# A hybrid encoder block on one core: keys taken in pairs, the second pass held back, expert rows spaced anew

## The chip, the core and the metric

The kernel runs on one core of a Trainium2 chip. The metric is the device time of one execution in microseconds (us). The engines are named as the profile names them: TensorE is PE (its weight loads PEld), VectorE is DVE, ScalarE is ACT, GpSimd is POOL, and SyncE (SP) issues most transfers.

## What is computed

The reference, cut to its frame (one layer, 1024 tokens of 1024 columns, 256 memory tokens, all float32):

```python
x = x + hybrid_mixer(rmsnorm(x))               # gated delta rule, 4 heads | RG-LRU, 512 channels
x = x + memory_cross_attention(rmsnorm(x), rmsnorm(mem))
x = x + peer_ffn(rmsnorm(x))                   # below
out = rmsnorm(x)

q = (t @ wq).reshape(ntok, 8, 2, 128)          # peer_ffn: 8 heads, two half queries
sc = einsum('thpd,hpkd->thpk', q, subkeys)     # 128 sub-keys per half
s1, i1 = top_k(sc[:, :, 0], 16); s2, i2 = top_k(sc[:, :, 1], 16)
best, pos = top_k(all sums of s1 and s2, 16)   # 16 experts per head, 128 per token
idx = e1 * 128 + e2; gate = softmax(best)
out = sum over the 128 experts of gate * gelu(u_tab[idx] . t) * v_tab[idx]
```

The expert tables `u` and `v` have 16384 rows of 4 KB each.

## The kernel before

**Two ways to the experts.** For 512 of the tokens (256 to 767) the kernel goes through all experts densely: a gate matrix G (token x expert, mostly zero) is built, then for each of 128 keys j (128 experts each) the `hidden(j)` step multiplies the tokens with `u`, applies gelu and the gates, and the `out(j)` step multiplies the result with `v` into PSUM. float32 products are made as three products of a high and a low part (`split`, `mm3`): ACT casts the high part (`uh`, `vh`, `dah`), DVE subtracts it (`ul`, `vl`, `dal`). The other 512 tokens, in four blocks of 128, fetch their experts: `fetch()` issues an indirect transfer on POOL that brings one expert row of 4 KB to each of 128 tokens (tile `rb`, 6 places), and `step()` lets DVE work on it (one pass over 128x1024: a dot product for `u`, a scaled sum for `v`). There are 4 blocks x 128 experts x 2 tables = 1024 such steps, called expert rows here.

**Stages.** The mixers run in four passes of 256 tokens (`heads`: projections, convolutions, the RG-LRU; `delta`: the chunked delta rule, a chain of small products). The units of `attend` (0, 128, 256, 512, 768) follow as their tokens are done: cross attention, the expert query, scores (16 rounds of `top16`), then `choose`/`select`, which gives the expert numbers `idx`. When the mixers are over, `gates` builds G for the dense tokens: per four tokens DVE writes two one-hot tiles (`oh1`, `oh2`), ACT scales one by the gates (`ohg`), PE multiplies them (`gd`), ACT copies to `stage`, and each 16 tokens a transfer of 1 MB writes `stage` to memory. The rest of `attend` runs beside it. Then the dense stage runs alone with the expert rows that are left.

**What sets the order.** `together` interleaves these streams by ranks and by a planner's clock while the program is written; each engine then runs its instructions in that order. PE's hook `tick` calls `step()` once per `pe.pace` nanoseconds of planned PE time, but not while DVE is planned more than `SLACK` behind or the oldest row has not landed: `PACES` are the spacings in the four passes, `PACE_G` that of the gates stage, and in the dense stage the rows that are left are spread evenly (`DENSE / rows left`). In `heads` a pass starts its projections when the pass before has finished its RG-LRU:

```python
while prev and "y" not in prev.ready:
    yield None
```

**The dense stage.** PSUM has one bank for `dh` (the hidden product), six for the outputs of three token blocks, and one (`po3`) for the fourth block, which is used for two keys and half the columns at a time (`last(0)`, `last(1)` in `out` of an odd key) and each time added to `acc` by DVE before PE may write the bank again. G lies as [128 experts, 512 tokens, 8 keys], so the gates of one key are read with a stride of 8 floats.

Of the kernel before, what the change touches and what calls it, by code (L numbers as in the profile page):

```python
# [8 lines left out]
F = mybir.dt.float32  # L9
BF = mybir.dt.bfloat16  # L10
FR = mybir.dt.float32r
I32 = mybir.dt.int32
U32 = mybir.dt.uint32
AF = mybir.ActivationFunctionType
# [9 lines left out]
TD = 2 * T  # L24
EC = 8
# [11 lines left out]
HOP, SLACK, WAIT = 100.0, 8000.0, 1000.0  # L37
SHARE = (6.0, 1.0, 6.0, 1.0)
L_NORM, L_STEP, L_CONV, L_SOFT, L_GATE = 14000.0, 2500.0, 4000.0, 6000.0, 1500.0
PACES = (2800.0, 2800.0, 2800.0, 3500.0)  # L40
PACE_G, DENSE = 3500.0, 1316000.0
FIRST = 0
EARLY = T
UNITS = ((0, 1), (128, 1), (256, 2), (512, 2), (768, 2))
# [5 lines left out]
def block_kernel(ctx: ExitStack, tc: tile.TileContext, a):  # L50
# [76 lines left out]
    act, dve = Engine(nc.scalar, 200.0, 0.72), Engine(nc.vector, 68.0, 1.04)  # L127
# [296 lines left out]
    def heads(fp, P, prev, qkv):  # L424

        t0, ready = P.t0, P.ready
# [11 lines left out]
        def tmp():  # L438
            return fp.tile([128, T], F, name="cy", bufs=CB)

        while prev and "y" not in prev.ready:
            yield None
        pe.pace = PACES[t0 // T]
        hT = fp.tile([128, 8, T], F, name="hT", bufs=1)
# [330 lines left out]

    done = {}
    read, chosen = set(), set()


    def attend(fp, t0, nb, KT, VM):  # L780
# [72 lines left out]
        for r in range(16):  # L853
            qT = ahead
            if r < 15:
                ahead = yield from query(r + 1)
            yield [qT]
            sk = fp.tile([128, 128], F, name="subk", bufs=2)
            sp.dma_start(sk, a["subk"][r])
            sc = bank("sc", 2)  # L860
            for b in range(nb):
                pe.matmul(sc[:, b * 128:(b + 1) * 128], qT[:, b * 128:(b + 1) * 128], sk,
                          start=True, stop=True)
            sc = sc.rearrange("p (b k) -> p b k", b=4)
            for b in range(nb):
                top16(fp, s12[b][:, r, :], i12[b][:, r, :], sc[:, b, :], 128)
            yield 0

        def choose():
            if not t0:  # L870
# [162 lines left out]
    def u_raw(p, j):  # L1033
        raw = p.tile([128, D], F, name="ur", bufs=2)
        sp.dma_start(raw, a["ut"][j])
        return raw

    def v_raw(p, j):
        raw = p.tile([128, D], F, name="vr", bufs=2)
        sp.dma_start(raw, a["v"][j * 128:(j + 1) * 128, :])  # L1040
        return raw

    def dense(p1, p, ps, hT, raws):
        hhi, hlo = hT
        NT = TD // 128
        res = [[ps.tile([128, 512], F, name=f"po{t}{d}") for d in range(2)] for t in range(NT - 1)]
        acc = p.tile([128, D], F, name="acc", bufs=1)
        row3 = D0 + TD - 128
        sp.dma_start(acc, x2d[row3:row3 + 128, :])

        def split(raw, name, bufs):
            hi = p1.tile([128, D], FR, name=name + "h", bufs=bufs)
            lo = p1.tile([128, D], FR, name=name + "l", bufs=bufs)
            act.copy(hi, raw)
            dve.tensor_sub(lo, raw, hi.bitcast(F))
            return hi, lo

        G = [None]
        A, V = {}, {}

        def hidden(j):
            if j % EC == 0:
                G[0] = p.tile([128, TD, EC], F, name="G", bufs=2)
                sp.dma_start(G[0], gd[j // EC])
            u, v = raws.pop(0) if raws else (u_raw(p1, j), v_raw(p1, j))
            uh, ul = [c8(t) for t in split(u, "u", 2)]
            V[j] = split(v, "v", 3)
            h = ps.tile([128, TD], F, name="dh")
            for c in range(8):
                mm3(h, (uh[:, c, :], ul[:, c, :]), (hhi[:, c, :], hlo[:, c, :]), c == 0, c == 7)  # L1070
            g = p.tile([128, TD], F, name="dg", bufs=2)
            act.activation(g, h, AF.Gelu_apprx_tanh)
            dve.tensor_mul(g, g, G[0][:, :, j % EC])
            ah = p.tile([128, TD], FR, name="dah", bufs=3)
            al = p.tile([128, TD], FR, name="dal", bufs=3)
            act.copy(ah, g)
            dve.tensor_sub(al, g, ah.bitcast(F))
            A[j] = (ah, al)

        xs = []  # L1080

        def add_res(t):
            x = xs[0][:, t, :]
            for d in range(2):
                ds = slice(d * 512, (d + 1) * 512)
                dve.tensor_add(x[:, ds], x[:, ds], res[t][d])
            finish(x, D0 + t * 128, xs[0][:, NT - 1, :])

        def out(j):
            def part(o, i, t, d, start, stop):  # L1090
                ts, ds = slice(t * 128, (t + 1) * 128), slice(d * 512, (d + 1) * 512)
                mm3(o, [x[:, ts] for x in A[i]], [x[:, ds] for x in V[i]], start, stop)

            def last(d):
                o = ps.tile([128, 512], F, name="po3")
                for i in (j - 1, j):
                    part(o, i, NT - 1, d, i < j, i == j)
                ds = slice(d * 512, (d + 1) * 512)
                dve.tensor_add(acc[:, ds], acc[:, ds], o)

            if j == 124:
                xs.append(p.tile([128, TD, EC], F, name="G", bufs=2).rearrange("p (t d) k -> p t (d k)", t=4))
                sp.dma_start(xs[0][:, 0:NT - 1, :],
                             x2d[D0:row3, :].rearrange("(t p) m -> p t m", p=128))
            if j % 2:
                last(0)
            for t in range(NT - 1):
                for d in range(2):
                    part(res[t][d], j, t, d, j == 0, j == 127)
                if j == 127:  # L1110
                    add_res(t)
            if j % 2:
                last(1)
                for i in (j - 1, j):
                    A.pop(i), V.pop(i)

        hidden(0)
        for j in range(128):
            if j + 1 < 128:
                hidden(j + 1)  # L1120
            for _ in range(LATE):
                next(late[0], None)
            out(j)
        finish(acc, row3, xs[0][:, NT - 1, :])
# [161 lines left out]
    def attended():  # L1286
        yield from memory(att, KT, VM)
        first.rank = FIRST
        for t0, nb in UNITS:
            while t0 not in done:  # L1290
                yield None
            yield from attend(att, t0, nb, KT, VM)
        while D0 + TD - T not in begun:
            yield None
        front.close()
        d1 = ctx.enter_context(tc.tile_pool(name="duv", bufs=1))
        dn.append(d1)
        raws.extend((u_raw(d1, j), v_raw(d1, j)) for j in range(2))

    dn, hT, raws, begun = [], [], [], set()  # L1300
    wp = front.enter_context(tc.tile_pool(name="wp", bufs=1))
    att = front.enter_context(tc.tile_pool(name="att", bufs=1))
    KT = att.tile([128, 8, MEM], F, name="KT")
# [4 lines left out]
    with tc.tile_pool(name="dn", bufs=1, side="right") as d2, \  # L1308
            tc.tile_pool(name="dps", bufs=1, space=bass.MemoryType.PSUM) as dps:
        pe.pace, pe.real = DENSE / (2.0 * (S - TD) - stepped[0]), False  # L1310
        dense(dn[0], d2, dps, hT, raws)
    while step():
        pass

# [63 lines left out]
```

## Time and profile before

| | us |
|---|---|
| median of 3 runs | 3226.76 (3224.28 to 3238.54) |
| the profiled execution, its own time | 3238.51 |
| its span, first to last instruction | 3236.7 |
| span up to the first expert row, about | 430 |
| mixers with expert rows, up to the gates stage | 430 to 1305 |
| gates stage | 1305 to 1743 |
| dense stage, first to last product | 1743 to 3223 |

A window of the profile gives, for each engine, its busy time and in brackets the number of its instructions that began there; PEclk is the granted TensorE clock as a share of full speed. "A <- B" in a list of waits means that A stood idle until B was done.

### The profile page before, as it was taken

What the parts mean: (1) busy time and instruction counts of PE and PEld (TensorE: products, weight loads), DVE (VectorE), ACT (ScalarE), POOL (GpSimd) and SP (SyncE); (2) the same over time, 40 slices, a digit from 0 to 9 for tenths busy, and PEclk for the clock granted to TensorE, in tenths of its full rate; (3) what the DMA queues carried; (4) which work ended last, traced back from release to release, by engine and by line L of the source; (5) the groups of instructions that cost most, each with busy time, mean ns of one, the idle gap of its engine ahead of it and who ended that gap; (6) DMA issues with size and microseconds to landing.
All of it is one profiled execution on the core that took longest, in us unless ns stands there. A gap on an engine that the chain in (4) does not pass through costs nothing.

```text
span 3236.7 us, 46492 instructions
## 1 busy us (share of the span) xinstructions
PE 2982.7 (92%) x16212; PEld 2554.5 (79%) x16212; DVE 2723.6 (84%) x5999; ACT 1281.2 (40%) x2694; POOL 1454.7 (45%) x1046
## 2 busy tenths in 40 slices
PE   7899899899999889888667999999999999999998
PEld 6889888888898788777566778778877778788786
DVE  7652578888786987999997999888999999899999
ACT  6844264255315531656575322222222232222222
POOL 0000023245232443343423776666666666666673
PEclk9999999999999999998778999999999999999999
DMA  5244769888787778889978899999999989999996
GB/s 172 92 150 144 228 235 323 307 303 307 274 293 252 249 284 303 295 302 302 308 249 289 303 354 326 339 325 342 355 350 339 344 313 360 325 343 353 345 347 211
DMA packets 321547, 941.66 MB, mean 291 GB/s; under 512 B 28912, under 2 KB 108832, under 8 KB 319264
## 3 DMA queue, kind: packets, MB, share of 16 engines
q0 software_dynamic: 148048, 538.04, 46.8%
q1 hardware_dynamic: 107216, 367.08, 31.5%
q10 hardware_dynamic: 66048, 33.56, 3.7%
q8 instruction: 128, 2.10, 0.3%
q14 instruction: 107, 0.88, 0.1%
HBM read 894.53 MB, written 44.04 MB: 290 GB/s over the span
## 4 chain that ended last, share of the span: by engine, by line
PE 49%; DVE 25%; DMA 12%; issue 7%; ACT 5%; POOL 2%; SPq 0%; another core or an unknown queue 0%; DVEq 0%; POOLq 0%; ACTq 0%
PE dh L108 15%; PE po L108 14%; PE pj L108 14%; DVE rb L83 8%; PE gd L108 4%; DMA rb<-in_v,idx 4%; DVE oh L83 3%; DMA gd<-stage 2%; POOL rb L1157 2%; DMA rb<-in_u,idx 2%; PE tp L113 1%; DVE i L83 1%; DMA w<-in_pwq 1%; PE sc L108 1%; DVE dg L83 1%
## 5 line engine op out<-in xcount | busy, mean ns | idle before, releaser
L1157 POOL DMA_INDIRECT rb<-in_u,idx x512 | 701.2, 1369 | 1104.2 <-DVE lxf L83 419.7
L1157 POOL DMA_INDIRECT rb<-in_v,idx x512 | 744.5, 1454 | 638.8 <-DVE rb L83 429.7
L83 DVE SCALAR_TENSOR_TENSOR rb<-rb,ga 128x1024 f32<-128x1024 f32 x512 | 655.8, 1281 | 29.5 <-DMA rb<-in_v,idx 23.9
L83 DVE SCALAR_TENSOR_TENSOR rb<-rb 128x1024 f32<-128x1024 f32 x512 | 611.2, 1218 | 31.4 <-DMA rb<-in_u,idx 31.3
L108 PE MATMUL pj<-hT,w 128*128 128x256 f32 (+1 forms) x2880 | 591.4, 357 | 16.0 <-DMA w<-in_pwq 14.4
L108 PEld LDWEIGHTS pj<-hT,w 128*128 128x128 f32 x2880 | 491.0, 195 | 70.8 <-DMA w<-in_pwq 14.5
L108 PE MATMUL po<-vh,dah 128*128 128x512 f32 x1024 | 408.5, 399 | 27.7 <-DVE acc L83 27.7
L108 PE MATMUL dh<-hT_h,uh 128*128 128x512 f32 x1024 | 409.9, 400 | 7.6 <-ACT dg L83 6.9
L108 PE MATMUL dh<-hT_h,ul 128*128 128x512 f32 x1024 | 408.3, 399 | 2.1 <-DVE ul L83 2.1
L108 PE MATMUL dh<-hT_l,uh 128*128 128x512 f32 x1024 | 408.5, 399 | 0.0
L108 PE MATMUL po<-vl,dah 128*128 128x512 f32 x1024 | 408.1, 399 | 0.0
L108 PE MATMUL po<-vh,dal 128*128 128x512 f32 x1024 | 406.8, 398 | 0.0
L83 ACT CAST uh<-ur 128x1024 fp32r<-128x1024 f32 x128 | 134.7, 1053 | 602.2 <-PE dh L108 399.8
L108 PE MATMUL gd<-ohg,oh 128*128 128x128 f32 x1024 | 182.7, 335 | 83.3 <-ACT ohg L83 66.1
L108 PEld LDWEIGHTS po<-vh,dah 128*128 128x128 f32 x1024 | 193.4, 189 | 80.4 <-DVE acc L83 33.4
L108 PEld LDWEIGHTS gd<-ohg,oh 128*128 128x128 f32 x1024 | 165.9, 234 | 99.7 <-ACT ohg L83 91.8
L108 PEld LDWEIGHTS dh<-hT_h,uh 128*128 128x128 f32 x1024 | 195.2, 191 | 56.2 <-ACT dg L83 7.8
L108 PEld LDWEIGHTS dh<-hT_h,ul 128*128 128x128 f32 x1024 | 194.4, 190 | 50.6 <-DVE ul L83 2.9
L108 PEld LDWEIGHTS dh<-hT_l,uh 128*128 128x128 f32 x1024 | 195.0, 190 | 47.4
L108 PEld LDWEIGHTS po<-vl,dah 128*128 128x128 f32 x1024 | 193.8, 189 | 47.1
L108 PEld LDWEIGHTS po<-vh,dal 128*128 128x128 f32 x1024 | 193.7, 189 | 46.8
L83 ACT CAST dah<-dg 128x512 fp32r<-128x512 f32 x128 | 79.6, 622 | 305.1 <-DVE dg L83 302.4
(341 smaller groups left out, 4806.0 us busy)
## 6 DMA issues: line engine op xcount, KB each, us to landing
ur<-in_ut SPq DMA_DIRECT2D x128, 512.0 KB
vr<-in_v SPq DMA_DIRECT2D x128, 512.0 KB
w<-in_wA SPq DMA_DIRECT2D x80, 512.0 KB
w<-in_pwq SPq DMA_DIRECT2D x80, 512.0 KB
gd<-stage ACTq DMA_DIRECT2D x32, 1024.0 KB
G<-gd SPq DMA_DIRECT2D x16, 2048.0 KB
w<-in_wout SPq DMA_DIRECT2D x40, 512.0 KB
w<-in_wq SPq DMA_DIRECT2D x40, 512.0 KB
```

The costliest lines, as they stand in the source:

```text
L83: r = call(*args, **kw)
L108: self.engine.matmul(out, l, r, **kw)
L113: self.engine.transpose(out, i, ident)
L1157: pool.indirect_dma_start(out=t, out_offset=None, in_=a[ph], in_offset=bass.IndirectOffsetOnAxis(ap=B["idx"][:, k:k + 1], axis=0))
```

## The change

Three edits:

1. Keys in pairs: the gelu of two neighbouring keys is written side by side (`dg` is [512 tokens, 2]), and the product with G, the cast `dah` and the difference `dal` are made once per pair. `hidden` now runs two keys ahead of `out`, and the split of `v` is a step of its own (`values`), one key ahead.
2. The expert rows' spacing: 2800, 2800, 2800, 3500 ns become 2500, 2500, 2500, 3000 in the passes, and 3500 becomes 5000 in the gates stage.
3. The projections of the second pass wait until some unit has had its 16 rounds of scores (`asked`), which is the first unit (token 0).

```diff
-PACES = (2800.0, 2800.0, 2800.0, 3500.0)
-PACE_G, DENSE = 3500.0, 1316000.0
+PACES = (2500.0, 2500.0, 2500.0, 3000.0)
+PACE_G, DENSE = 5000.0, 1316000.0
...
-        while prev and "y" not in prev.ready:
+        while prev and ("y" not in prev.ready or not asked):
             yield None
...
+    asked = set()
...
                 top16(fp, s12[b][:, r, :], i12[b][:, r, :], sc[:, b, :], 128)
             yield 0
+        asked.add(t0)
...
-            u, v = raws.pop(0) if raws else (u_raw(p1, j), v_raw(p1, j))
+            u = raws.pop(0) if raws else u_raw(p1, j)
             uh, ul = [c8(t) for t in split(u, "u", 2)]
-            V[j] = split(v, "v", 3)
...
-            g = p.tile([128, TD], F, name="dg", bufs=2)
-            act.activation(g, h, AF.Gelu_apprx_tanh)
-            dve.tensor_mul(g, g, G[0][:, :, j % EC])
-            ah = p.tile([128, TD], FR, name="dah", bufs=3)
-            al = p.tile([128, TD], FR, name="dal", bufs=3)
-            act.copy(ah, g)
-            dve.tensor_sub(al, g, ah.bitcast(F))
-            A[j] = (ah, al)
+            if j % 2 == 0:
+                g2[0] = p.tile([128, TD, 2], F, name="dg", bufs=2)
+            g = g2[0]
+            act.activation(g[:, :, j % 2], h, AF.Gelu_apprx_tanh)
+            if j % 2:
+                dve.tensor_mul(g, g, G[0][:, :, j % EC - 1:j % EC + 1])
+                ah = p.tile([128, 2, TD], FR, name="dah", bufs=2)
+                al = p.tile([128, 2, TD], FR, name="dal", bufs=2)
+                g = g.rearrange("p t k -> p k t")
+                act.copy(ah, g)
+                dve.tensor_sub(al, g, ah.bitcast(F))
+                for k in range(2):
+                    A[j - 1 + k] = (ah[:, k, :], al[:, k, :])
+
+        def values(j):
+            V[j] = split(rawv.pop(0) if rawv else v_raw(p1, j), "v", 3)
...
         hidden(0)
+        values(0)
+        hidden(1)
         for j in range(128):
             if j + 1 < 128:
-                hidden(j + 1)
+                values(j + 1)
+            if j + 2 < 128:
+                hidden(j + 2)
...
             out(j)
```

How the change moves instructions shows in the order in which each engine is given them. On PE, near the end of the first pass (before): `pj<-w,qkv` and `pj<-w,yl` are the first pass's output projection, `tp<-identf,qkv` transposes the second pass's input, and `c_wab` is the weight of that pass's first projection, so the second pass starts here.

```order
L108 MATMUL pj<-w,qkv 128x128 x4
L108 MATMUL pj<-w,yl 128x128 x4
L113 MATMUL tp<-identf,qkv 128x128 x2
L113 MATMUL tp<-identf,g_1947 128x128 x4
L108 MATMUL pj<-hT,c_wab 8x256
L113 MATMUL tp<-identf,qkv 128x128 x2
L108 MATMUL pj<-hT,c_wab 8x256
L113 MATMUL tp<-identf,qkv 128x128 x4
L108 MATMUL pj<-hT,c_wab 8x256
L113 MATMUL tp<-identf,qkv 128x128 x2
```

With the change the first pass's output projection is still under way at the last of the 16 score rounds of the first unit (`sc<-subk,pqT`):

```order
L108 MATMUL pj<-w,qkv 128x128 x4
L108 MATMUL pj<-w,yl 128x128 x4
L108 MATMUL sc<-subk,pqT 128x128
L113 MATMUL tp<-identf,qkv 128x128
L108 MATMUL pj<-w,qkv 128x128 x4
```

and the second pass's first projection follows 14 rows later:

```order
L108 MATMUL pj<-w,yl 128x128 x4
L113 MATMUL tp<-identf,qkv 128x128 x4
L108 MATMUL pj<-hT,c_wab 8x256
L113 MATMUL tp<-identf,qkv 128x128 x2
L108 MATMUL pj<-hT,c_wab 8x256 x7
```

So all 16 score rounds now stand ahead of the second pass's projections, where eight of these projections stood ahead of the first round.

On DVE in the gates stage (before), where `oh<-iot` and `oh<-keys` are the two one-hot tiles of four tokens and `rb,hdot<-rb` is an expert row of `u`:

```order
L83 SCALAR_TENSOR_TENSOR rb,hdot<-rb 128x1024 x6
L83 TENSOR_TENSOR oh_14367<-iot,e1T 128x512
L83 TENSOR_TENSOR oh_14368<-keys,e2T 128x512
L83 SCALAR_TENSOR_TENSOR rb,hdot<-rb 128x1024
L83 TENSOR_TENSOR oh_14384<-iot,e1T 128x512
L83 TENSOR_TENSOR oh_14385<-keys,e2T 128x512
L83 SCALAR_TENSOR_TENSOR rb,hdot<-rb 128x1024 x2
L83 TENSOR_TENSOR oh_14403<-iot,e1T 128x512
L83 TENSOR_TENSOR oh_14404<-keys,e2T 128x512
L83 TENSOR_TENSOR oh_14419<-iot,e1T 128x512
L83 TENSOR_TENSOR oh_14420<-keys,e2T 128x512
L83 SCALAR_TENSOR_TENSOR rb,hdot<-rb 128x1024 x3
```

About the same one-hot tiles with the change (`MAX`, `MAX_INDEX` and `MATCH_REPLACE` on `cand` belong to a `select`, which is planned at another place than before; `rb<-rb,ga` is an expert row of `v`):

```order
L83 TENSOR_TENSOR oh_14489<-iot,e1T 128x512
L83 TENSOR_TENSOR oh_14490<-keys,e2T 128x512
L83 MAX best<-cand 128x8 x2
L83 MAX_INDEX pos<-best,cand 128x8
L83 MATCH_REPLACE mr_15621<-best,cand 128x80
L83 MAX_INDEX pos<-best,cand 128x8
L83 TENSOR_TENSOR oh_14505<-iot,e1T 128x512
L83 TENSOR_TENSOR oh_14506<-keys,e2T 128x512
L83 SCALAR_TENSOR_TENSOR rb<-rb,ga 128x1024
L83 TENSOR_TENSOR oh_14521<-iot,e1T 128x512
L83 TENSOR_TENSOR oh_14522<-keys,e2T 128x512
L83 SCALAR_TENSOR_TENSOR rb<-rb,ga 128x1024
```

Where 12 expert rows stood among four pairs of one-hot tiles, two stand among three. Counted over the whole order, 274 expert rows stood ahead of the first one-hot tile and 131 between it and the first `dg`; now it is 352 and 84 (436 ahead of the first `dg`, where it was 405), and 588 are left for the dense stage instead of 619.

On DVE in the dense stage (before), most of a period of two keys: two `dg` of 512 elements, two `dal`, two `acc`, and the expert rows between them.

```order
L83 TENSOR_TENSOR ul<-ur,uh 128x1024 x2
L83 TENSOR_TENSOR dg<-dg,G 128x512
L83 TENSOR_TENSOR acc<-acc,po_19053 128x512
L83 SCALAR_TENSOR_TENSOR rb,hdot<-rb 128x1024
L83 TENSOR_TENSOR dal<-dg,dah 128x512
L83 SCALAR_TENSOR_TENSOR rb,hdot<-rb 128x1024 x2
L83 TENSOR_TENSOR acc<-acc,po_19083 128x512
L83 TENSOR_TENSOR vl<-vr,vh 128x1024
L83 SCALAR_TENSOR_TENSOR rb,hdot<-rb 128x1024 x3
L83 TENSOR_TENSOR vl<-vr,vh 128x1024
L83 TENSOR_TENSOR dg<-dg,G 128x512
L83 SCALAR_TENSOR_TENSOR rb,hdot<-rb 128x1024
```

With the change the period has one `dg` and one `dal`, of 1024 elements each:

```order
L83 TENSOR_TENSOR ul<-ur,uh 128x1024 x2
L83 TENSOR_TENSOR dg<-dg,G 128x1024
L83 TENSOR_TENSOR acc<-acc,po_19003 128x512
L83 SCALAR_TENSOR_TENSOR rb,hdot<-rb 128x1024
L83 TENSOR_TENSOR dal<-dg,dah 128x1024
L83 SCALAR_TENSOR_TENSOR rb,hdot<-rb 128x1024
L83 TENSOR_TENSOR acc<-acc,po_19035 128x512
L83 TENSOR_TENSOR vl<-vr,vh 128x1024
L83 SCALAR_TENSOR_TENSOR rb,hdot<-rb 128x1024 x3
L83 TENSOR_TENSOR vl<-vr,vh 128x1024
```

Both `dg` and `dal` of the pair now stand beside `out` of the odd key, and the second half of the period, behind the second `vl`, holds expert rows alone.

## Rows read from the trace of the kernel before

**Rows 1.** The page, whole kernel: busy time, share of the span and instructions by engine.
```profile
PE 2982.7 (92%) x16212; PEld 2554.5 (79%) x16212; DVE 2723.6 (84%) x5999; ACT 1281.2 (40%) x2694; POOL 1454.7 (45%) x1046
```

**Rows 2.** Windows of three stages: mixers, gates, dense (columns in its head).
```profile
core 0: us, PE busy (x) PEld busy (x) DVE busy (x) ACT busy (x) POOL busy (x), PEclk, DMA share, GB/s
...
430.00:1305.00 875.00, 818.14 (x5370) 742.09 (x5369) 708.25 (x2188) 360.14 (x878) 324.49 (x282) 0.98 0.82 290
1305.00:1743.00 438.00, 336.16 (x1898) 302.12 (x1897) 402.26 (x1275) 283.35 (x767) 165.22 (x130) 0.85 0.88 290
1743.00:3223.00 1480.00, 1447.31 (x6120) 1158.16 (x6120) 1362.46 (x1624) 416.69 (x529) 956.92 (x614) 0.99 0.91 333
```

**Rows 3.** The same windows, VectorE's instructions on tile rb alone (the expert rows).
```profile
430.00:1305.00 875.00, 342.08 (x422) 0.98 0.82 290
1305.00:1743.00 438.00, 158.66 (x240) 0.85 0.88 290
1743.00:3223.00 1480.00, 777.61 (x881) 0.99 0.91 333
```

**Rows 4.** Waits in the dense stage, 1760 to 3200 us: engine, waited for, total, times, longest.
```profile
PE po L108 <- DVE acc L83: 27.7, 11, 5.0
DVE rb L83 <- DMA rb<-in_u,idx: 22.2, 9, 6.0
DVE rb L83 <- DMA rb<-in_v,idx: 20.6, 12, 4.8
```

**Rows 5.** Timeline of VectorE around a late expert row: start, length, instruction, idle before.
```profile
2124.08 1.22 DVE L83 SCALAR_TENSOR_TENSOR rb<-rb 128x1024 f32<-128x1024 f32 x1 [5.01 <-DMA rb<-in_u,idx]
...
2129.77 0.68 DVE L83 TENSOR_TENSOR acc<-acc,po 128x512 f32<-128x512 f32 x1
```

**Rows 6.** Timeline of TensorE at the same place.
```profile
2130.50 0.51 PE L108 MATMUL po<-vh,dah 128*128 128x512 f32 x1 [3.91 <-DVE acc L83]
```

**Rows 7.** Groups of VectorE's instructions by shape, whole kernel: count, busy, mean ns, idle.
```profile
L83 DVE SCALAR_TENSOR_TENSOR rb<-rb,ga 128x1024 f32<-128x1024 f32 x512 | 655.8, 1281 | 29.5 <-DMA rb<-in_v,idx 23.9 <-issue 0.2
L83 DVE SCALAR_TENSOR_TENSOR rb<-rb 128x1024 f32<-128x1024 f32 x512 | 611.2, 1218 | 31.4 <-DMA rb<-in_u,idx 31.3
L83 DVE TENSOR_TENSOR vl<-vr,vh 128x1024 fp32r<-128x1024 f32 x128 | 155.9, 1218 | 2.6 <-ACT vh L83 2.6
...
L83 DVE TENSOR_TENSOR dg<-dg,G 128x512 f32<-128x512 f32 x128 | 151.9, 1188 | 1.0 <-ACT dg L83 0.8
L83 DVE TENSOR_TENSOR dal<-dg,dah 128x512 fp32r<-128x512 f32 x128 | 88.1, 689 | 1.4
...
L83 DVE TENSOR_TENSOR oh<-oh 128x128 bf16<-128x128 bf16 x32 | 8.9, 277 | 0.2
L83 DVE TENSOR_TENSOR e<-oh 128x64 f32<-128x64 bf16 x32 | 8.7, 272 | 0.3
```

**Rows 8.** Waits in the gates stage, 1305 to 1743 us.
```profile
PE gd L108 <- ACT ohg L83: 66.1, 44, 6.4
ACT ohg L83 <- DVE oh L83: 55.1, 36, 8.9
...
ACT stage L83 <- DMA gd<-stage: 16.7, 5, 8.2
```

**Rows 9.** Windows inside the mixers stage and one of the dense stage.
```profile
700.00:800.00 100.00, 94.38 (x525) 82.90 (x526) 80.66 (x192) 64.12 (x143) 53.79 (x44) 1.00 0.91 325
1000.00:1100.00 100.00, 90.44 (x539) 80.58 (x538) 88.15 (x302) 61.29 (x141) 34.89 (x29) 0.97 0.72 246
2200.00:2300.00 100.00, 100.00 (x430) 80.39 (x429) 92.09 (x132) 29.50 (x37) 66.98 (x44) 1.00 0.94 345
```

**Rows 10.** GpSimd's timeline where the first expert row is fetched.
```profile
429.56 1.00 POOL L1157 DMA_INDIRECT rb<-in_u,idx  x1 [419.72 <-DVE lxf L83]
```

**Rows 11.** Windows over the first unit's attention and scores.
```profile
270.00:320.00 50.00, 47.43 (x369) 44.43 (x369) 12.29 (x57) 21.58 (x75) 0.00 (x0) 0.97 0.47 150
320.00:430.00 110.00, 99.57 (x741) 93.02 (x741) 69.00 (x331) 33.70 (x97) 0.44 (x1) 0.98 0.63 204
```

More of the change, by code (lines that the diff above doesn't have):

```diff
@@ L1041, in v_raw, with dense @@
         return raw
-    def dense(p1, p, ps, hT, raws):
+    def dense(p1, p, ps, hT, raws, rawv):
         hhi, hlo = hT
@@ L1058, in dense @@
         G = [None]
-        A, V = {}, {}
+        A, V, g2 = {}, {}, [None]
         def hidden(j):
@@ L1297, in attended @@
         dn.append(d1)
-        raws.extend((u_raw(d1, j), v_raw(d1, j)) for j in range(2))
-    dn, hT, raws, begun = [], [], [], set()
+        for j in range(2):
+            raws.append(u_raw(d1, j))
+            rawv.append(v_raw(d1, j))
+    dn, hT, raws, rawv, begun = [], [], [], [], set()
     wp = front.enter_context(tc.tile_pool(name="wp", bufs=1))
@@ L1310, in block_kernel @@
         pe.pace, pe.real = DENSE / (2.0 * (S - TD) - stepped[0]), False
-        dense(dn[0], d2, dps, hT, raws)
+        dense(dn[0], d2, dps, hT, raws, rawv)
     while step():
```

## The prediction

> **What bounds the kernel now.** The page comes first [rows 1]: PE is busy 92% of the span and DVE 84%, so neither alone explains the time, and the stages have to be read apart. The windows by stage do that [rows 2]. In the dense stage (1743 to 3223 us) PE is busy 98%: it is PE's, with little to win. A window in which PE never waits holds 430 products in 100 us [rows 9]; the stage has 128 keys x 48 = 6144, so its floor is 6144 / 4.30 = 1429 us, and 1480 - 1429 = 51 us are lost. In the gates stage (1305 to 1743) PE is busy 77% at a granted clock of 0.85, DVE 402 of 438 us: it is DVE's. In the mixers (430 to 1305) PE is busy 94%, DVE 81%.
>
> Next, what the losses wait for. In the dense stage PE's largest wait is for `acc`, 27.7 us in 11 waits, and DVE itself waits 42.8 us for expert rows that have not landed [rows 4]. The two belong together: at 2124.08 a row starts 5.01 us late, the `acc` queued behind it starts at 2129.77 [rows 5], and PE, which needs the bank back, stands still for 3.91 us [rows 6]. DVE cannot catch up, since it is busy 1362.5 / 64 = 21.3 us of each 22.3 us that PE needs for a pair of keys. In the gates stage PE waits for ACT's `ohg` (66.1 us), ACT for DVE's one-hot tiles (55.1 us) [rows 8], and DVE spends 158.7 us of its 402 on expert rows [rows 3].
>
> **The change, part by part.** I take the terms against the profiled execution (3238.5 us, span 3236.7), which lies 11.7 us above the median of the runs, and carry the sum over to the median.
>
> *Pairs of keys.* Per pair DVE now makes two `dg` of 1.188 and two `dal` of 0.689 us, 3.75 us [rows 7]. The pair's two instructions cover 1024 elements each; the nearest such row is `vl` with 1.218 us, which gives 2.44, a saving of 1.32 us, 84 us over 64 pairs. The open point is whether strided reads run at that rate. `dg` costs 1.188 us for 512 elements where `dal`, read without gaps, costs 0.689: a single float every 32 bytes is read at half rate. Two rows of `select` price the pair: `oh<-oh 128x128` reads runs of two elements 32 bytes apart, 128 in 277 ns, and `e<-oh 128x64` single elements 32 bytes apart, 64 in 272 ns. So the run is paid, not the element, and pairs from G should come at the full rate. No row has floats at a stride of 8 bytes, as `dal` and `dah` now read them. Bounds: 1.218 us as `vl`, or twice `dg`, 2.38 us. I take the lower, since two such floats lie as close as the runs of two that cost nothing extra. In a window's busy time, instructions that overlap at their ends count once, so I count 75 of the 84 us. At the upper bound for both instructions DVE would gain 64 us of work instead.
>
> [...]
>
> ACT's `dah` becomes one cast instead of two and its gelu writes at a stride of 8 bytes; ACT is busy 417 of 1480 us in the stage [rows 2], which hides a doubling. `hidden` two keys ahead puts one product more ahead of the first `out`, work that PE has to do anyway. SP's queue now issues loads of `u` and `v` two by two. The `u` buffer comes free when its `ul` is done, and the load has a whole period less one product (over 11 us) to land, so I price the new queue order at nothing. It would cost if a load of `u` took longer than that.
>
> *The spacing.* Each expert row costs DVE 342 / 274 = 1.25 us in the mixers, 159 / 131 = 1.21 in the gates stage and 778 / 619 = 1.26 in the dense stage [rows 3], with the counts of the order.
>
> Dense stage: 31 rows less, 39 us. With the pairs, DVE's work is 1362 - 39 - 75 = 1248 us, 19.5 us per pair; its slack per pair grows from 1.0 to 2.8 us. A late row (21 waits of 2.0 us on average) is then caught up within a pair instead of two. PE's 11 waits of 2.5 us should shrink to about 0.7 us, 20 us less, and I add 8 us for the smaller losses of the stage that follow DVE: **-28 us**. Bounds: 0, at the upper price of the strided reads, to -45, if nearly all 51 us go.
>
> Gates stage: 47 rows less, 57 us of DVE's 402. At today's share of DVE (92%) the stage would take 345 / 0.92 = 376 us, -62. ACT's 283 us and the writes of `stage` (ACT waits 16.7 us for them) stay, so the share will fall; at 86% it is 401, -37. I take 89%, 387 us: **-51 us**. The products, the one-hot tiles and the order of their chain are unchanged.
>
> Mixers: 78 rows more, 97 us of DVE. They have room: DVE idles 167 us there, and the rows begin earlier, since the first unit's scores come ahead of the second pass's projections. Those are eight projections of about 3 to 4 us and their convolutions, so I put the first row, now at 429.6 us [rows 10], at about 375. DVE's load over 375 to 1305 is then some 89%. What it costs PE: nothing, or, if every 100 us became like the worst of the stage (1000 to 1100, PE 90.4% against 93.5% on average [rows 2, 9]), 3.1% of 930 = 29 us. I take **+15 us**. Queued behind a row on DVE are the convolutions and the chain of `delta`, for which PE waits in program order.
>
> *The hold.* It moves PE work and removes none; every projection runs later. Its price is cover: the first unit's norm, softmax and copies are chains during which PE did the second pass's projections. From 270 to 430 us PE idles 13 us in all [rows 11]. Without cover this may double; bounds 0 and +13, taken **+7 us**. The mixers as a whole end no later for it, since in the order the first gate product stands behind the same PE work as before.
>
> Sum: -28 - 51 + 15 + 7 = -57 us. Profiled execution 3181, median 3227 - 57 = **3170 us**.
>
> **Rivals.** *The whole gain, no price* (0.12): DVE's idle time takes all 78 rows and the hold costs nothing; gates at -62, dense at -45: 3227 - 107 = 3120 us. For it: 700 to 800 us holds 50 us of DVE's time in expert rows, 40 of them or one in 2.5 us, with PE still 94% busy [rows 9]. Against: the dense stage's waits for landing rows do not go away, since transfers stay at over 330 GB/s.
>
> *The gain goes back in the mixers* (0.14): rows at a spacing of 2.6 us instead of 3.2 delay the chain of `delta` as they now delay `ohg`, and PE's share falls from 93.5% to 88%: 5.5% of 930 is 51 us instead of 15, and with the strided reads at the upper price (dense at -10) the sum is -51 + 51 + 7 - 10 = -3: 3224 us. Against: from 1000 to 1100 us DVE is already at 88%, and PE is still at 90% [rows 9].
>
> *Slower, by transfers* (0.08). The mixers move 290 GB/s x 875 us = 254 MB. The 78 rows add 41 MB, the earlier start about 10, 305 MB in 930 us, 328 GB/s. If these small mixed transfers saturate at 290 GB/s, the stage takes 305 / 0.290 = 1052 us, +122 instead of +15, since the weights for the projections queue with the rows: 3227 + 122 + 7 - 51 - 28 = 3277 us. It decides below about 304 GB/s, where the stage's cost passes 72 us and the sum turns positive. Against: 325 GB/s at 700 to 800 us with PE at 94%, and 333 over the whole dense stage.
>
> **How the numbers follow.** The forecast has 0.66, with its own range 3140 to 3200 (dense -12 to -40, gates -37 to -62, mixers and hold 0 to +42). The median's own scatter is 0.4% of runs, so about 0.5%, 16 us, is what can be told from no change. Faster by more than that is below 3211: the forecast, the whole gain and a small part of the third case, 0.80. Within: most of the third case, 0.12. Slower: 0.08. The range 3128 to 3220 leaves out the slow case, half of the third and half of the whole gain, about 2 in 10.
>
> **What would show it.** Right: `dg` and `dal` of 128x1024 at about 1.22 us each, 64 of each; DVE's share in the dense stage at 86 to 88%, and PE's wait for `acc` under 12 us; the dense stage at 1445 to 1460 us; the gates stage at 376 to 401 us with the granted clock above 0.85; the first expert row fetched at 365 to 385 us; the gates stage beginning at 1310 to 1340 us. Wrong: `dal` at about 2.4 us (then the dense stage keeps its length); a gates stage of over 410 us (then ACT or the writes of `stage` bound it, not DVE); mixers that end after 1360 us with PE waiting for `w` or for `W` and `lxf` of DVE (then the rows moved there cost what they saved).

## The result, and the profile after

The changed kernel took 3216.79 us (median of 9 runs, 3207.01 to 3224.09), the one before, beside it, 3232.63 (9 runs). The ratio is 0.9944, 95% interval 0.9925 to 0.9963: some 16 us faster. The sign and the range held; the size did not, 57 us were forecast.

The stages of the profiled execution (own time 3218.09 us, span 3216.1) are read by the same three instructions in both kernels: the first product `gd<-ohg`, the first `dh`, and the last `po`.

| | before | after | forecast |
|---|---|---|---|
| first expert row | 429.6 | 371.2 | about 375 |
| first gate product | 1309.4 | 1380.0 (+71) | +22 |
| gates stage, to the first `dh` | 422.1 | 374.2 (-48) | -51 |
| dense stage, to the last `po` | 1490.9 | 1446.2 (-45) | -28 |
| end | 3222.4 | 3200.4 (-22) | -57 |

The first `dh` stands at 1731.5 us in the kernel before, ahead of the border at 1743 in [rows 2]. So its gates and dense stages come out as 422.1 and 1490.9 us here, not as 438 and 1480. The end moves by 22 us where the medians differ by 16, since the profiled execution of the kernel before lies 6 us above its median.

So two terms came in, one even better than forecast, and the mixers took most of it back. The windows of the changed kernel by stage (length, then busy time of PE, PEld, DVE, ACT and POOL with their instructions, granted clock, DMA share, GB/s), first all instructions and then DVE's on expert rows alone:

```profile
371.00:1380.00 1009.00, 904.66 (x5749) 808.86 (x5748) 819.76 (x2457) 381.59 (x956) 422.74 (x360) 0.96 0.84 300
1380.00:1754.00 374.00, 309.89 (x1850) 276.62 (x1850) 338.95 (x1108) 274.57 (x758) 104.90 (x79) 0.91 0.82 258
1754.00:3200.00 1446.00, 1438.14 (x6140) 1154.12 (x6141) 1264.69 (x1470) 421.89 (x472) 819.00 (x587) 1.00 0.91 333
...
371.00:1380.00 1009.00, 437.90 (x578) 0.96 0.84 300
1380.00:1754.00 374.00, 99.06 (x111) 0.91 0.82 258
1754.00:3200.00 1446.00, 741.71 (x853) 1.00 0.91 333
```

Against [rows 2, 3] PE's share of the mixers fell from 93.5% to 904.66 / 1009 = 89.7%, while DVE's is 81% as before. In the dense stage PE is busy 99.5% and DVE 87.5%. There the groups of DVE's instructions by shape (busy time, mean ns | idle before them) and PE's longest waits are:

```profile
L83 DVE TENSOR_TENSOR vl<-vr,vh 128x1024 fp32r<-128x1024 f32 x128 | 155.6, 1215 | 0.0
...
L83 DVE TENSOR_TENSOR dg<-dg,G 128x1024 f32<-128x1024 f32 x64 | 78.4, 1225 | 6.7 <-ACT dg L83 3.9 <-DMA ur<-in_ut 2.8
L83 DVE TENSOR_TENSOR dal<-dg,dah 128x1024 fp32r<-128x1024 f32 x64 | 77.9, 1217 | 3.9 <-ACT dah L83 3.8
...
PE dh L108 <- ACT dg L83: 2.8, 2, 2.0
PE po L108 <- DVE acc L83: 2.7, 3, 1.1
```

The pair's two instructions take what `vl` takes, and the wait for `acc`, 27.7 us in [rows 4], is 2.7.

Up to the first gate product PE has the same work in both kernels, 8214 and 8218 products. The windows up to there, the kernel before first (the same columns as above):

```profile
0.00:1309.40 1309.40, 1203.00 (x8214) 1097.64 (x8215) 953.72 (x3077) 581.75 (x1406) 332.53 (x302) 0.98 0.71 246
...
0.00:1380.00 1380.00, 1228.51 (x8218) 1110.56 (x8218) 1033.73 (x3241) 574.15 (x1392) 430.31 (x380) 0.96 0.74 261
```

PE is idle 106.4 us before and 151.5 after, busy 1203.0 and 1228.5: 45 of the 71 us are waiting, and 26 are the same products taking longer. Of its waits up to there those for ACT grew most, from 41.5 to 71.4 us; those for DVE grew from 36.5 to 47.4, those for transfers only from 27.5 to 30.1.

The loss in the mixers is not spread evenly. Of the windows of 10 us between the first expert row and the first gate product, PE is busy for less than 60% of one before (1080 us) and of seven after (520, 640, 650, 660, 850, 860 and 1140 us). At the longest of these places PE's timeline (start, duration, instructions, and in brackets the idle time before and who ended it) reads:

```profile
639.70 1.06 PE L108 MATMUL gd<-Y,W 128*128 128x128 f32 x8
640.60 1.10 PE L108 MATMUL gd<-Xi,TT 128*128 128x128 f32 x8
645.50 1.74 PE L108 MATMUL gd<-Y,W 128*128 128x128 f32 x8 [3.80 <-DVE W L83]
647.04 1.92 PE L108 MATMUL gd<-St,knT 128*128 128x128 f32 x8
652.18 2.25 PE L108 MATMUL gd<-g,Y 128*128 128x128 f32 x8 [3.23 <-DVE g L83]
655.11 2.08 PE L108 MATMUL gd<-Xi,kd 128*128 128x128 f32 x8 [0.67 <-ACT Xi L83]
656.98 1.92 PE L108 MATMUL gd<-St,qkv 128*128 128x128 f32 x8
660.12 1.16 PE L108 MATMUL gd<-Xi,g 128*128 128x128 f32 x8 [1.23 <-ACT go L83]
...
669.26 1.26 PE L113 MATMUL tp<-identf,go 128*128 128x128 f32 x4 [6.24 <-DVE go L83]
671.30 2.08 PE L108 MATMUL pj<-w,qkv 128*128 128x128 f32 x8 [0.78 <-ACT qkv L83]
```

Only the chain of `delta` stands on PE from 640 to 669 us, one link after the other, and PE waits for DVE at three of them. Ahead of `W` DVE works on four expert rows (639.75 to 644.53 us). The cost is paid twice: besides the waits, groups of eight products that take 1.06 us take up to 2.25. The windows of these stretches show the granted clock:

```profile
640.00:650.00 10.00, 5.15 (x31) 4.69 (x30) 10.00 (x30) 1.66 (x3) 7.64 (x4) 0.83 0.49 141
650.00:660.00 10.00, 5.91 (x24) 5.16 (x24) 10.00 (x45) 2.83 (x9) 8.08 (x7) 0.66 0.88 308
660.00:670.00 10.00, 3.37 (x16) 2.13 (x16) 8.62 (x47) 4.29 (x18) 2.42 (x3) 0.82 0.54 181
670.00:680.00 10.00, 8.77 (x51) 8.24 (x51) 10.00 (x21) 1.73 (x2) 6.48 (x5) 0.67 0.78 261
680.00:690.00 10.00, 9.92 (x89) 9.76 (x88) 8.38 (x19) 1.04 (x1) 5.78 (x6) 1.00 1.02 394
```

PE is idle for 15.6 of the 30 us from 640 to 670, the granted clock is 0.66 to 0.83 in the four windows from 640 to 680, and from 680 it is at 1.00. DVE meanwhile is busy 28.6 of the 30 us: expert rows, the selection of the second unit, and the links of the chain between them.

### The profile page after: what moved, and what is told of

It is laid out like the page before. It is cut to its first block, busy times and chain, and to the rows that moved or that the text cites. A ratio compares the mean times of both kernels' runs of the same rounds, so it can differ in the third digit from the quotient of the medians.

```text
span 3216.1 us, 46207 instructions
## 1 busy us (share of the span) xinstructions
PE 2977.8 (93%) x16212; PEld 2542.0 (79%) x16212; DVE 2649.2 (82%) x5871; ACT 1274.1 (40%) x2627; POOL 1354.2 (42%) x1046
## 4 chain that ended last, share of the span: by engine, by line
PE 54%; DVE 18%; issue 10%; DMA 8%; ACT 4%; POOL 4%; SPq 0%; POOLq 0%; ACTq 0%; DVEq 0%
PE pj L108 16%; PE po L108 16%; PE dh L108 16%; DVE rb L83 6%; POOL rb L1172 4%; PE gd L108 4%; DVE oh L83 3%; DMA rb<-in_u,idx 2%; PE tp L113 1%; DMA w<-in_pwq 1%; DMA subk<-in_subk 1%; PE sc L108 1%; DMA w<-in_wo 1%; DMA rb<-in_v,idx 1%; DVE i L83 1%
## 5 line engine op out<-in xcount | busy, mean ns | idle before, releaser
L1172 POOL DMA_INDIRECT rb<-in_u,idx x512 | 668.0, 1305 | 1063.0 <-DVE hist L83 372.9
L1172 POOL DMA_INDIRECT rb<-in_v,idx x512 | 677.2, 1323 | 759.7 <-DVE rb L83 531.4
L83 DVE TENSOR_TENSOR ul<-ur,uh 128x1024 fp32r<-128x1024 f32 x128 | 155.9, 1221 | 125.5 <-ACT uh L83 125.3
L108 PE MATMUL gd<-ohg,oh 128*128 128x128 f32 x1024 | 171.6, 316 | 55.9 <-ACT ohg L83 35.4
L108 PEld LDWEIGHTS gd<-ohg,oh 128*128 128x128 f32 x1024 | 153.3, 211 | 74.3 <-ACT ohg L83 70.1
```

Source lines behind the costliest of these rows:

```text
L83: r = call(*args, **kw)
L108: self.engine.matmul(out, l, r, **kw)
L1172: pool.indirect_dma_start(out=t, out_offset=None, in_=a[ph], in_offset=bass.IndirectOffsetOnAxis(ap=B["idx"][:, k:k + 1], axis=0))
```

## The experiments

Two theories to begin with. *Rows*: the denser expert rows hold up the chains on DVE. *Hold*: the held projections are cover that is missing later. The first four kernels undo parts of the change: the first undoes the hold and the spacing, the second the hold alone, the third the spacing alone, the fourth the spacing in the mixers alone.

```diff
-        while prev and ("y" not in prev.ready or not asked):
+        while prev and "y" not in prev.ready:
...
-PACES = (2500.0, 2500.0, 2500.0, 3000.0)
-PACE_G, DENSE = 5000.0, 1316000.0
+PACES = (2800.0, 2800.0, 2800.0, 3500.0)
+PACE_G, DENSE = 3500.0, 1316000.0
```

**The pairs alone.**

> The pairs alone: the hold and the new spacing are undone. Neither theory of the mixers touches this run; it measures the dense term by itself. DVE has 618 rows in the dense stage instead of 588. Mixers and gates stage as before (first gate product at about 1310 us, dense from about 1743), the dense stage at 1450 to 1460 us instead of 1480. Expected: 3205 to 3213 us. If the pairs alone bring nothing, 3225 or more, the dense gain of the changed kernel came from its 31 fewer rows.

3197.75 us, ratio 0.9909 (0.9893 to 0.9924). The dense stage takes 1459.0 us, 32 less with 615 rows fetched in it against 614 before: that is the pairs' own worth. The other 13 us of the changed kernel's dense stage come with fewer rows (587). The time is below the expected 3205, with the first gate product at 1297.7 us in this profile, not at 1310. The pairs alone are also faster than the changed kernel (0.9909 against 0.9944): its other two edits together cost some 19 us.

**Without the hold.**

> The changed kernel without the hold; pairs and new spacing stay. In the changed kernel the first gate product comes 71 us later than before. Theory rows: the denser expert rows on DVE delay the chains for which PE waits; then the delay stays, the first gate product is at 1360 to 1375 us and the time is 3205 to 3217 us. Theory hold: the held projections are PE work that later has no other stream beside it, so that short chains stand uncovered; then the first gate product is at 1310 to 1330 us and the time 3160 to 3175 us.

3219.21 us, ratio 0.9966 (0.9954 to 0.9978); first gate product at 1384.8 us. Undoing the hold brings nothing; theory rows seems to stand, though both numbers lie a little above what it had said.

**The hold without the spacing.**

> The changed kernel with the spacing of before in all stages; pairs and hold stay. Theory rows: the first gate product comes at 1310 to 1330 us, the gates stage takes about 435 us, the dense stage about 1450: 3205 to 3225 us. Theory hold: the first gate product at 1360 to 1380 us, the rest as above: 3255 to 3270 us, slower than before the change.

3203.85 us, ratio 0.9921 (0.9908 to 0.9935); first gate product at 1325.0 us, gates stage 419, dense stage 1444.7 with 596 rows. Kernels without the hold and with the old spacing in the mixers have it at 1297.7 to 1311.2 us (three profiles), so the hold, with the order that it brings, costs 14 to 27 us. It does not cost them where the prediction looked: from 270 to 430 us PE idles 12 us here and 10 in the changed kernel, 13 before. The rows that it starts early return part of that in the dense stage.

**The hold with the wider gates alone.**

> The changed kernel with the spacing of before in the mixers and the new, wider one in the gates stage; pairs and hold stay. DVE has 646 rows in the dense stage. Theory rows: first gate product at 1310 to 1330 us, gates stage about 380, dense stage 1455 to 1460: 3155 to 3180 us. Theory hold: first gate product at 1360 to 1380 us, the rest as above: 3210 to 3225 us.

3204.0 us, ratio 0.9921 (0.9903 to 0.9939). First gate product at 1323.2, gates stage 371.2, but the dense stage takes 1488.4 us with 645 rows: what the gates stage gains there goes back. Neither theory had that.

**Which side of a row costs.** Two kernels without the hold and with the new spacing make the rows of the mixers light, on DVE or in the transfer, and a third does both:

```diff
+            c = 64 if pe.mix else D
+            behind(row_pass([t, t, B["h"], B["hd"][:, k:k + 1]], t[:, :c], t[:, :c], 1.0, B["h"][:, :c],
...
+        c = 8 if pe.mix else 128
...
-            out=t, out_offset=None, in_=a[ph],
-            in_offset=bass.IndirectOffsetOnAxis(ap=B["idx"][:, k:k + 1], axis=0))
+            out=t[:c], out_offset=None, in_=a[ph],
+            in_offset=bass.IndirectOffsetOnAxis(ap=B["idx"][:c, k:k + 1], axis=0))
```

`row_pass` emits the short pass and books the full one. Where the transfers are light, the passes for `u` in the mixers also multiply with 0 instead of 1, so that what is left in the row buffers does not grow.

> Without the hold, with the new spacing (first gate product at 1385 us, against 1298 with the pairs alone). In the mixers each expert row is still fetched whole, but DVE's pass over it covers 64 of its 1024 columns, so the output lacks the rest; the planner books the full pass, and the order of PE's instructions is all but the same. DVE sheds about 320 of its 802 us there. Theory queue (PE's chains wait behind rows on DVE): first gate product at 1270 to 1310 us. Theory transfers (the rows' bytes delay the weights): 1365 to 1385 us. Theory order (the new spacing interleaves the streams in a worse order, and the rows themselves cost nothing): 1360 to 1385 us.

> The same kernel, no hold and new spacing. In the mixers DVE makes the full pass over each expert row, but the transfer brings rows for 8 of the 128 tokens, so the other tokens' rows are missing from the output; a fill of the row buffers with zeros takes DVE some 7 us once. The order of PE's instructions is the same. The 336 rows of the mixers move 11 MB instead of 176. Theory transfers: first gate product at 1300 to 1320 us. Theories queue and order: 1375 to 1395 us.

> Both of the last two edits together: in the mixers an expert row is a transfer for 8 tokens and a pass over 64 columns. What is left of the delay then is the order of PE's instructions alone. Theory order: first gate product still at 1355 to 1380 us. Theories queue and transfers: 1260 to 1300 us, below the run with the pairs alone (1298), since the 274 rows there cost something too.

The first gate product is at 1345.8, 1329.7 and 1297.2 us, against 1384.8: 39 us for DVE's passes, 55 for the bytes, 88 for both. Each is one profile. Theories queue and transfers each hold for a part, though neither as far as it had said, and with both taken away nothing is left for order alone. With light transfers PE waits for no transfer at all in the mixers; in the kernel without the hold and with full rows these are its waits of that kind (us in total, times, longest), 21.9 of the 55 us:

```profile
PE pj L108 <- DMA w<-in_pwq: 10.6, 2, 10.0
...
PE sc L108 <- DMA subk<-in_subk: 6.7, 5, 2.1
...
PE pj L108 <- DMA w<-in_wo: 3.3, 2, 2.9
...
PE pj L108 <- DMA w<-in_wout: 1.3, 1, 1.3
```

**Fewer rows, and the price of one.**

> The pairs alone, with a wider spacing in the mixers: 3200, 3200, 3200, 4000 ns instead of 2800, 2800, 2800, 3500. 35 rows move from the mixers to the dense stage. If a row in the mixers costs about 1 us of the end, as the runs with closer rows say, the first gate product comes 30 to 50 us earlier, at about 1260 us, and the dense stage takes 25 to 35 us more: 3185 to 3200 us. If the price of a row rises only past the old spacing, the mixers gain under 15 us and the time is 3210 to 3225 us.

3243.27 us, ratio 1.0038 (1.0023 to 1.0052). Both times miss. With 42 rows fewer the first gate product comes at 1303.8 us, no earlier, as the second guess had it for the mixers, and the dense stage takes 1488.0, 29 more, as both had it. What neither had is the gates stage: 434.2 us, 17 more than the pairs alone, since 64 products of a unit's expert query and 16 of its scores now stand behind the first gate product. A price per row does not explain that.

**The light rows at the old spacing, and in the changed kernel.**

> The pairs alone, at the old spacing, with the expert rows of the mixers made light as in the run with both edits (transfers for 8 tokens, passes over 64 columns; the rest is missing from the output). With full rows the first gate product is at 1298 us here and at 1385 with the new spacing; with light rows at the new spacing it was at 1297. Theory steep price: the rows cost little at the old spacing and much past it, and the order of PE's instructions is worth little; then this run has its first gate product at 1270 to 1297 us. Theory order: a row costs the same everywhere, 88 us / 336 = 0.26 us, and the new spacing interleaves the streams worse; then it is at 1220 to 1240 us, some 60 us before the light run at the new spacing.

> The changed kernel (hold and new spacing) with the same light rows in the mixers. With full rows its first gate product is at 1380 us. If the rows are what the mixers lose, it is at 1280 to 1305 us, no later than without the hold (1297). If the hold costs PE cover by itself, whatever the rows do, it is at 1315 to 1345 us.

With light rows the first gate product is at 1296.3 us at the old spacing, where full rows have 1297.7 to 1311.2: there the rows cost 15 us at most. In the changed kernel it is at 1364.1: light rows return 16 of the 71 us, although DVE's load in the mixers falls from 81% to 51%. So the rows are the smaller part of what the changed kernel loses. What is left is the hold and the order in which the planner interleaves the streams, since it books DVE's time for rows and goes by it.

**Between the two spacings.**

> The pairs alone, with a spacing in the mixers between the old and the new: 2650, 2650, 2650, 3250 ns. 23 rows move from the dense stage to the mixers; the dense stage takes 1446 to 1452 us instead of 1459. Theory order with a flat price of 0.26 us: the mixers lose 6 us, or whatever the new order brings; 3190 to 3205 us. Theory steep price, 87 us / 62 rows = 1.4 us each: the mixers lose about 32 us: 3215 to 3230 us.

3221.84 us, ratio 0.997 (0.9953 to 0.9987); first gate product at 1313.4, dense stage 1447.7 as expected, but the gates stage takes 435 us. The time comes out as theory steep price has it, the mixers do not: here too the 80 products of a unit stand behind the first gate product. The first `dh`, behind all of this work, is 33 us later than with the pairs alone. But this kernel has an order of its own, so it does not tell rows from order.

**Order and rows apart.** The picks of `together` are recorded from one kernel and played back in another:

```diff
+SEQ = ...        # one stream's number for each pick
-        while live:
-            ready = [c for c in live if c.at <= pe.at]
...
+        for turn_of in SEQ:
+            c = IDS[turn_of]
```

> The pairs, no hold, the new spacing, but the streams interleaved in the order recorded from the kernel with the pairs alone (first gate product at 1298 us; the new spacing with its own order had it at 1385). Theory order: a row costs 0.26 us, 62 more rows cost 16, first gate product at 1305 to 1325 us, the gates stage 355 to 365, the dense stage (613 rows) 1459: 3140 to 3165 us, faster than every kernel so far. Theory rows: first gate product at 1365 to 1385 us and 3200 to 3220 us in all.

> The changed kernel (pairs, hold, new spacing), but the streams interleaved in the order recorded from the kernel with pairs, hold and old spacing (first gate product at 1325 us). Theory order: first gate product at 1330 to 1345 us, gates stage 375, dense stage 1446: 3165 to 3185 us. Theory rows: 1370 to 1385 us, 3205 to 3220 us in all, as the changed kernel with its own order.

> The reverse: pairs, hold and the old spacing, but the streams interleaved in the changed kernel's order. Theory order: first gate product at 1355 to 1380 us although the rows are as few as before, gates stage 420, dense stage 1446: 3235 to 3260 us, slower than before. Theory rows: 1320 to 1340 us and 3200 to 3220 us.

First gate products, us:

| order recorded from | rows at the old spacing | rows at the new spacing |
|---|---|---|
| no hold, old spacing | 1297.7 | 1343.1 |
| no hold, new spacing | | 1384.8 |
| hold, old spacing | 1325.0 | 1351.9 |
| hold, new spacing (the changed kernel) | 1368.5 | 1380.0 |

The kernels at 1297.7, 1384.8, 1325.0 and 1380.0 us run in their own order, the others in a recorded one. Down a column only the order changes: 42, 28 and 43 us. Along a line only the rows change: 45, 27 and 12 us. The third kernel came out as theory order had it, the first two between the theories: both are right in part. Three profiles with no hold and the old spacing in the mixers differ by 13 us (1297.7 to 1311.2), so the 12 is not to be told from nothing.

An order also decides how much other work stands ahead of the first gate product. With the order of the pairs alone 32 rounds of `select` on `cand` fall into the gates stage, in the kernel without the hold 20, and its gates stage is shorter (355 us against 371). At the first `dh`, behind all of that work, the order makes 25 us (1739.9 and 1714.5), 23 (1754.2 and 1731.3) and 31 (1775.2 and 1744.2); by the ratios of the times it makes 40, 24 and 41 us. So an order is worth 23 to 43 us, whichever way it is measured.

The changed kernel's order with rows at the old spacing is slower than the kernel before (3251.61 us, ratio 1.0047, 1.0029 to 1.0064); its rows in the better order give 3194.46 (0.9871, 0.9838 to 0.9904). Without the hold, the new spacing in the old order takes **3183.51 us, ratio 0.9843 (0.9815 to 0.9870)**, the lowest median of all, 33 us under the changed kernel; its interval overlaps that of the kernel with 3194.46.

What an order does is seen at the chain shown above. This is the same part of it, the third `gd<-St,knT`, in the kernel with the hold and the old spacing:

```profile
612.21 1.06 PE L108 MATMUL gd<-St,knT 128*128 128x128 f32 x8
613.10 0.39 PE L108 MATMUL sc<-subk,pqT 128*128 128x128 f32 x2
613.33 1.95 PE L108 MATMUL pj<-hT,w 128*128 128x128 f32 x16
615.11 1.06 PE L108 MATMUL gd<-g,Y 128*128 128x128 f32 x8
616.00 0.39 PE L108 MATMUL sc<-subk,pqT 128*128 128x128 f32 x2
616.23 1.95 PE L108 MATMUL pj<-hT,w 128*128 128x128 f32 x16
618.01 1.06 PE L108 MATMUL gd<-Xi,kd 128*128 128x128 f32 x8
```

Between two links stand the expert query and the scores of another unit, so PE waits at none of these, and products keep to 1.06 us. The same link in the kernel before, and in the one with the changed kernel's rows but this order:

```profile
606.32 1.06 PE L108 MATMUL gd<-St,knT 128*128 128x128 f32 x8
607.21 0.39 PE L108 MATMUL sc<-subk,pqT 128*128 128x128 f32 x2
607.44 1.95 PE L108 MATMUL pj<-hT,w 128*128 128x128 f32 x16
...
617.51 1.06 PE L120 MATMUL gd<-St,knT 128*128 128x128 f32 x8
618.64 0.46 PE L120 MATMUL sc<-subk,pqT 128*128 128x128 f32 x2
618.94 1.95 PE L120 MATMUL pj<-hT,w 128*128 128x128 f32 x16
```

And in the kernel with the old spacing's rows but the changed kernel's order:

```profile
643.83 1.52 PE L123 MATMUL gd<-Y,W 128*128 128x128 f32 x8 [3.72 <-DVE best L98]
645.14 1.91 PE L123 MATMUL gd<-St,knT 128*128 128x128 f32 x8
647.79 2.25 PE L123 MATMUL gd<-g,Y 128*128 128x128 f32 x8 [0.73 <-DVE g L98]
...
664.87 1.26 PE L128 MATMUL tp<-identf,go 128*128 128x128 f32 x4 [6.25 <-DVE go L98]
```

The links lie bare again, with fewer rows, and they are covered with more rows in the other order: the place belongs to the order. In the changed kernel the unit's query and scores were over by 635 us, before these links.

**An even price, and the wider gates.** The last two keep the best order and move rows only:

> The pairs, no hold, the order of the pairs alone played back, spacing 2650, 2650, 2650, 3250 ns in the mixers and 5000 beside the gates. About 25 more rows in the mixers than at the old spacing, 640 rows in the dense stage. Even price, 45 / 51 = 0.88 us a row: first gate product at 1317 to 1325 us. Price that rises late: 1298 to 1308 us. Gates stage 372 us, dense stage 1470 to 1485 us: 3175 to 3200 us.

> The same with the old spacing in the mixers: only the gates stage is spaced wider, 662 rows in the dense stage. First gate product at 1293 to 1303 us, gates stage 370 us, 47 less than the pairs alone; the dense stage at 0.9 us a row 1459 + 42 = 1500 us: 3185 to 3205 us, as the pairs alone (3198). If the dense stage has room for the rows, it stays under 1475 us and the time is 3160 to 3175 us.

First gate products at 1312.0 and 1311.2 us. The second has the mixers of the pairs alone (1297.7), so one profile of this point can be 13 us off another. The first lies between its two guesses. Against 1311.2 its 22 more rows in the mixers (304 fetched there, not 282) cost nothing, against 1297.7 they cost 14 us; the next 29 cost 31 us. That the price rises late is likely, but not shown. The times are 3193.61 us (0.9872, 0.9850 to 0.9895) and 3208.98 (0.9909, 0.9891 to 0.9929). Moving rows from the gates stage to the dense stage is worth nothing by itself (the ratio of the pairs alone was 0.9909 too): the gates stage falls from 417.1 to 373.6 us, the dense stage grows from 1459.0 to 1510.0. The windows of the dense stage in the two kernels, and PE's wait in the second:

```profile
1684.00:3174.00 1490.00, 1452.55 (x6141) 1158.66 (x6141) 1329.38 (x1529) 420.63 (x472) 907.52 (x641) 0.99 0.92 343
```

```profile
1685.00:3195.00 1510.00, 1461.85 (x6142) 1162.07 (x6143) 1351.98 (x1567) 420.88 (x473) 940.32 (x661) 0.99 0.93 345
...
PE po L120 <- DVE acc L95: 34.6, 27, 3.3
```

With 585 to 596 rows fetched in it the dense stage takes 1445 to 1448 us in five kernels; with 611 to 615 it takes 1450 to 1468, with 641 to 651 it takes 1488 to 1490, with 661 it takes 1510. Up to about 600 rows cost it nothing, beyond that some 1 us each, and the wait for `acc` comes back. One kernel stands apart: the old spacing's rows in the changed kernel's order, with 593 rows and 1462.4 us, where PE waits 9.3 us for `acc` and 7.7 for `dg`; so the number of rows alone does not settle it.

## Why the prediction was right in sign and wrong in size

*Pairs of keys*: right. `dal`, which reads one operand at a stride of 8 bytes, takes 1217 ns against `vl`'s 1215, and `dg`, which reads G in pairs, takes 1225 ns for 1024 elements where it took 1188 for 512 [rows 7]. That floats 8 bytes apart are read as fast was an estimate, by the bf16 rows of `select` [rows 7]; the 1217 ns of `dal` show it for this kernel. DVE's share of the stage, the wait for `acc` and the stage's length all came where the list of signs put them.

*Dense stage, -28*: it was -45, the edge of the bounds. The pairs alone gave 32, and the fewer rows gave the rest, since they take the stage under the 600 rows up to which it is PE's alone (busy 99.5%). There was luck in that: with -28 the time would have been some 3234 us, no faster than the kernel before and outside the range.

*Gates stage, -51*: it was -48, with the granted clock at 0.91, and its 374.2 us lie just under the 376 to 401 of the list of signs. PE's wait for `ohg` fell from 66.1 us [rows 8] to 35.4.

*Mixers, +15 and hold, +7*: here it failed; they cost 71. The step that failed is "What it costs PE: nothing, or, if every 100 us became like the worst of the stage (...), 3.1% of 930 = 29 us", and beside it "The mixers as a whole end no later for it, since in the order the first gate product stands behind the same PE work as before". The work is the same, as the counts of products show, but it takes 71 us longer. By the runs these are 16 us for the hold with its order (14 to 27 by the other profiles), 28 to 43 for the new order and 12 to 27 for the rows: 16 + 28 + 27 or 16 + 43 + 12, by the two ways through the table, against the profile of before. The hold was under-sized by a factor of two or more, and its bound of 13 as well. The rows lie within their bounds of 0 and 29. The order had no term: I read from the order that the same work stood ahead of the first gate product, and took that to mean that it would take as long. That the spacing moves the planner's clock for DVE, and with it the choice of what stands between the links of `delta`, had no place in the sum; a bound by the worst window of the kernel before cannot hold such a term, since there the links were covered, as at 606 us.

Of the signs of being wrong the time came, 1380 us where it named 1360, but not the waits. For `w`, `W` and `lxf` together PE waited 34.2 us up to the first gate product before and 32.4 after.

*The rivals*: the time came nearest to the second, the gain that goes back in the mixers (3224 us), though by other terms: it has the mixers and the hold at 58 us and the dense stage at -10. Its mechanism, rows that delay the chain of `delta`, is what the waits at 640 to 669 us show, but it asks for bare links, and these came with the order. The numbers of the rival by transfers look as if it had come: the mixers moved 300 GB/s, below the 304 at which it decides, and lost 71 us, where it has 72. But with light rows, at 130 GB/s, the changed kernel's first gate product is still at 1364.1 us, PE's waits for transfers grew by 2.6 us in all, and the fastest kernel moved 308 GB/s. Without the hold the bytes do cost 55 us.

Open: why the order without the hold loses 88 us to full rows and the changed kernel's order only 16. Both have bare links (without the hold PE waits 5.24 us at 527 us and 6.91 us at 653); which of them meet a late weight or a full DVE was not taken apart. Of the changed kernel's places with an idle PE only the one at 640 us was followed to its cause, and why its waits for ACT grew most is not shown.

## What to carry to other kernels

Where a planner orders the program by booked time, a change to background work is also a change of the order, and the second can cost as much as the first: compare what stands between the links of the longest chain, not only what stands ahead of a point. Record the order and play it back to tell the two apart; here that also gave the fastest version. Work that is moved out of one stage is worth what the receiving stage has left, so find each stage's threshold (here some 600 rows in the dense stage) before moving anything. And where edits come together, measure each by itself: here the first alone was faster than all three.

## What the hardware showed that was not expected

In these traces an operand with a float every 8 bytes costs DVE nothing extra (`dal`, 1217 ns for 1024 elements, `vl` 1215 without gaps), and ACT little: its `dah` of 1024 such elements takes 1129 ns, its `uh` of 1024 without gaps 1052. The chain that left PE half idle from 640 to 670 us took longer than its waits: some of its links ran in a window with a granted clock of 0.66 (650 to 660 us), with 2.08 us for eight products instead of 1.06.
